# A hybrid decoder layer on one core: v buffers with names of their own, more u units in the selection, another order at both ends, and a decay mask on ScalarE and VectorE

## The chip, the cores and the metric

The kernel runs on one core of a Trainium2 chip. The metric is the time of one execution on the device in microseconds (us). A profile of one execution goes with it: a span from the first to the last instruction, and a record of each instruction on the engines PE (TensorE; PEld is its weight load), DVE (VectorE), ACT (ScalarE), POOL (GpSimd) and on the DMA queues, of which SP (SyncE) issues nearly all loads.

## The reference

One decoder layer in float32 on 512 tokens of width 1024:

```python
n = rmsnorm(x)                                   # one projection feeds both mixers
h = x + W_out @ concat(gla(n), ssd(n))           # gated linear attention; Mamba-2 SSD
n2 = rmsnorm(h)
# PEER: 8 heads, product keys 128 x 128 = 16384 experts, the top 16 per head
q  = n2 @ w_query;  best 16 of each key half, then best 16 of their 256 sums, gate = softmax
h += sum_e gate[e] * gelu(n2 . u[e]) * v[e]
y  = rmsnorm_final(h)

# in ssd, per chunk of 128 tokens and per head
a_cum = cumsum(dt * A)
Lmat  = exp(where(causal, a_cum[l] - a_cum[s], -inf))     # the decay matrix
y_diag = ((C @ B.T) * Lmat) @ (X * dt)
```

## The kernel before

Each engine runs its instructions in the order in which the program was written, so the order of the code is the schedule. Where precision asks for it, an operand is split into a rounded high part and the rest: `split` (L102 to L104) makes the high part on ACT and the rest on DVE or, on request, on POOL, and `mm3` (L108 to L110) does three matmuls with the parts.

The stages, with their place in the profile:

- **Start (0 to 16 us).** The tokens are normalised (`scale`, L242; the power on POOL, L235), transposed (L266) and multiplied with 23 blocks of `w_in` that arrive one after another as `wraw`. `ahead` splits a block early.
- **Mixers (16 to 225 us).** In the SSD part `ssd_a(t)` makes, for each of 4 chunks and two groups of 4 heads, the decay matrix `lm`: matmuls with `selH` (L566) spread the cumulated decay over a PSUM bank, one matmul of `identr` with `negm` (L568) adds a large negative number above the diagonal, and ACT takes the exponential with a bias for each head (L571, `b<-pm,RT` in the profile). DVE then multiplies `lm` with the scores `psc` (L602, `b<-b,pm`), and `ssd_b(t)` uses it on PE (L614).
- **Query and selection (to 466 us).** DVE sorts out the top 16 of 16 and builds one-hot tables: `select` has chains of `tensor_tensor` on f16, which read and write `gat`. PE in the meantime does u units: one unit (`u_run(1)`) is 24 matmuls of a 128-expert block of `uT` with the tokens, whose raw block `ur` is loaded by SP and split by ACT and, in this stage, by POOL (`ul<-ur,uh`). `spread` transposes the indices on PE.
- **Gate stage (466 to 656 us).** 48 units `gunit`, 8 tokens each, make the dense gate matrix with one-hot matmuls from tables `A`, `eq`, `B` that DVE builds (L1186, `pg<-B,A`). The gates of the first 59 expert blocks stay in the `ring`; those of the others go to DRAM (`gd`) from the tile `stage`, 64 tokens at a time, by six DMAs on ACT's queue (L1199). The u units that are left are spread over these units in eight parts each, split on ACT and DVE: 33 units before.
- **V stage (to 1487 us).** One step for each of 128 expert blocks `e`: load v (`vr`, four buffers) and split it, split the gated activations of the ring slot (`hh`, `hl`), multiply, and do one u unit for a later block. `gload` refills a ring slot from `gd`. 256 gathers for the last 128 tokens are threaded in on POOL.
- **End.** `final()` (L1257 to L1320) adds the residuals and applies the last norm, four tiles of 128 tokens, to the output.

Which engine waits for a buffer is decided by the tile pools: a tile whose address was used by another tile waits for the last user of that one. The loads at the change from the gate stage to the V stage stand in this order:

```python
vs = Stream(self, vp, "v", [...], 4)
HT[0] = htile()
vs.loads(1)          # v blocks 0 and 1
u_run(1)
vs.split(1)
hprep(0)
u_run(1)
vs.loads(3)
...
gload(RS)            # first ring refill
```

Of the kernel before, what the change touches and what calls it, by code (L numbers as in the profile page):

```python
# [35 lines left out]
class Stream:  # L36
# [10 lines left out]
    def loads(s, upto):  # L47
        while s.nl <= min(upto, len(s.src) - 1):
            s.raw[s.nl] = s.c.tile([128, 1024], F32, name=s.nm + "r", bufs=s.nraw)
            s.y.load(s.raw[s.nl], s.src[s.nl])  # L50
            s.nl += 1
# [12 lines left out]
class Layer:  # L64
# [67 lines left out]
    def mixers(self):  # L132
# [125 lines left out]
        scale(2, 1, False)  # L258
        scale(3, 0, True)
# [7 lines left out]
        for dc in range(8):  # L267
            if dc == 0:
                ahead(0, 3, 0)
            act(nh[dc], px[dc], AF.Copy, scale=wmix[:, dc:dc + 1])  # L270
            stt(nl[dc], px[dc], wmix[:, dc:dc + 1], nh[dc].bitcast(F32), OP.mult, OP.subtract)
            if dc == 4:
                ahead(0, 3, 1)
        negm = c.tile([128, 128], F32R, name="negm")
        identr = c.tile([128, 128], F32R, name="identr")
        V.tensor_copy(negm, negm0)
        V.tensor_copy(identr, ident)
# [56 lines left out]
        def dts():  # L334
# [20 lines left out]
            V.tensor_scalar(R[32:40, :], ac, -1.0, None, op0=OP.mult)  # L355
# [9 lines left out]
        nacT = lambda t: RT[:, t, 32:40]  # L365
# [193 lines left out]
        def ssd_a(t):  # L559
            ts = slice(t * 128, (t + 1) * 128)  # L560
            lm = b4(F32, (128, 8, 128))
            for g in range(2):
                p = pt()
                for j in range(4):
                    h = 4 * g + j
                    T.matmul(p[:, j * 128:(j + 1) * 128], selH[:, h:h + 1].to_broadcast([40, 128]), acs[:, ts],  # L566
                             start=j == 0, stop=False, skip_group_check=True)
                T.matmul(p, identr, bc(negm, 1, 4), start=False, stop=True, skip_group_check=True)  # L568
                for j in range(4):
                    h = 4 * g + j  # L570
                    act(lm[:, h, :], p[:, j * 128:(j + 1) * 128], AF.Exp, bias=nacT(t)[:, h:h + 1])  # L571
# [27 lines left out]
            for g in range(2):  # L599
                r = slice(g * 64, g * 64 + 64)  # L600
                T.matmul(psc[g][:, :128], XB[4][r, ts], XB[5][r, ts], start=True, stop=True)
                tt(lm[:, 4 * g:4 * g + 4, :], lm[:, 4 * g:4 * g + 4, :], bc(psc[g][:, :128], 1, 4), OP.mult)  # L602
# [255 lines left out]
    def experts(self):  # L858
# [237 lines left out]
        select(1)  # L1096
        spread(0)
        u_run(1)
# [10 lines left out]
        u_run(4)  # L1109
# [124 lines left out]
        vs.loads(1)  # L1234
# [4 lines left out]
        vs.loads(3)  # L1239
# [15 lines left out]
        gload(RS)  # L1255

        def final():  # L1257
# [3 lines left out]
            junk = [c.tile([128, D], F32, name="gat", tag="gat", bufs=3), vp.tile([128, D], F32, name="vr", bufs=4)]  # L1261
# [26 lines left out]
            def scale(t):  # L1288
                stt(hs[t], hs[t], v[t][:, 3:4], wf, OP.mult, OP.mult)
                load(self.out[t], hs[t])  # L1290
# [9 lines left out]
            scale(3)  # L1300
            mean(0)
            power(0)
            residual(1, 0)
            weight(1, 0, G)
            residual(1, 1)
            weight(1, 1, G)
            scale(0)
            mean(1)
            power(1)
            residual(2, 0)  # L1310
            weight(2, 0, G)
            residual(2, 1)
            weight(2, 1, V)
            act(hs[1], hs[1], AF.Copy, scale=v[1][:, 3:4])
            load(self.out[1], hs[1])
            mean(2)
            power(2)
            act(hs[2][:, hf[0]], hs[2][:, hf[0]], AF.Copy, scale=v[2][:, 3:4])
            V.tensor_scalar(hs[2][:, hf[1]], hs[2][:, hf[1]], v[2][:, 3:4], None, op0=OP.mult)
            load(self.out[2], hs[2])  # L1320

        for e in range(NE):
# [8 lines left out]
            vs.loads(e + 4)  # L1331
# [15 lines left out]
            for i in range(3):  # L1347
                vgrp(0, i)
                if i == 2:
# [3 lines left out]
                    gload(e + 1 + RS)  # L1353
# [3 lines left out]
            for i in range(3):  # L1357
# [5 lines left out]
                fill(3 + i)  # L1363
            u_part(7)
            fill(6)
            if e == NE - 12:
                for t in (0, 1):
                    hs[t] = us.c.tile([128, D], F32, name="ur", bufs=2)
                    load(hs[t], self.hd[t])
# [99 lines left out]
```

## Time and profile before

| what | value |
|---|---|
| three runs, us | 1506.76, 1508.53 (median), 1512.19 |
| the profiled execution, us | 1503.02 |
| its span, us | 1501.2 |
| mean granted TensorE clock | 0.991 |
| busy, us: PE, PEld | 1456.2, 1278.0 |
| busy, us: DVE, ACT, POOL | 1169.4, 632.7, 451.7 |
| chain that ended last | PE 80%, DVE 12%, issue 3%, DMA 2%, ACT 2% |

The span lies 1.8 us under the execution's own time. Busy times of engines lie beside each other, and matmuls are pipelined, so the duration of a matmul in a row is longer than its distance to the next one. The chain is followed back from the last instruction, at each step to what released it.

### The profile page before, as it was taken

The numbers are of one execution on the slowest core, as the hardware profiler recorded it, in microseconds if no ns is written. First come the engines' busy times: TensorE is split into PE (matmuls) and PEld (weight loads), VectorE is DVE, ScalarE is ACT, GpSimd is POOL, SyncE is SP. The second block draws the span as 40 slices with busy tenths as digits, with TensorE's granted clock in tenths as the row PEclk, the third lists the DMA queues.
The fourth block names the chain that finished last, engine by engine and source line by source line (L and its number), as shares of the span: only waits on it lengthen the run. The fifth ranks groups of instructions, "written<-read, shape, count | busy, mean of one in ns | idle before, by whom it ended". The sixth has DMA issues, their size and how long they took to land.

```text
span 1501.2 us, 22402 instructions
## 1 busy us (share of the span) xinstructions
PE 1456.2 (97%) x7904; PEld 1278.0 (85%) x7904; DVE 1169.4 (78%) x2473; ACT 632.7 (42%) x1201; POOL 451.7 (30%) x380
## 2 busy tenths in 40 slices
PE   7999999999898999979999999999999999999997
PEld 5787778888898999878999999999999998888886
DVE  6542663789999999967877778777788888888886
ACT  5435633433654544433333333333333333444444
POOL 2002404444672000002333333333333333333332
PEclk9999999999999999999999999999999999999999
DMA  5231224222334556658888888889899888888894
GB/s 189 84 126 58 71 73 155 96 85 85 105 104 143 159 167 175 180 181 300 322 316 316 323 312 307 317 305 332 304 331 322 314 316 276 292 300 299 297 325 178
DMA packets 148738, 335.56 MB, mean 224 GB/s; under 512 B 64640, under 2 KB 73872, under 8 KB 148496
## 3 DMA queue, kind: packets, MB, share of 16 engines
q1 hardware_dynamic: 58672, 186.32, 36.1%
q0 software_dynamic: 36864, 134.23, 25.1%
q10 hardware_dynamic: 53088, 13.57, 3.9%
q8 instruction: 62, 1.02, 0.3%
q14 instruction: 52, 0.43, 0.1%
HBM read 315.79 MB, written 18.28 MB: 223 GB/s over the span
## 4 chain that ended last, share of the span: by engine, by line
PE 80%; DVE 12%; issue 3%; DMA 2%; ACT 2%; POOL 0%; SPq 0%; DVEq 0%; POOLq 0%; ACTq 0%
PE pm L109 25%; PE pm L108 25%; PE pm L110 25%; DVE gat L97 4%; PE pg L1186 2%; DVE B L97 1%; DVE ul L104 1%; PE pm L904 1%; DMA gd<-stage 1%; DVE ring L97 1%; DMA ur<-in_uT 1%; DVE eq L97 1%; DVE A L97 1%; ACT b L91 0%; ACT tp L91 0%
## 5 line engine op out<-in xcount | busy, mean ns | idle before, releaser
L108 PE MATMUL pm<-nT,uh 128*128 128x384 f32 (+1 forms) x1152 | 402.1, 349 | 8.8 <-ACT uh L91 8.3
L110 PE MATMUL pm<-nT,ul 128*128 128x384 f32 (+1 forms) x1152 | 397.0, 345 | 2.0 <-POOL ul L104 2.0
L109 PE MATMUL pm<-nT,uh 128*128 128x384 f32 (+1 forms) x1152 | 397.0, 345 | 0.5 <-DVE nT L97 0.5
L109 PE MATMUL pm<-vl,hh 128*128 128x512 f32 x765 | 300.4, 393 | 0.2 <-DVE vl L104 0.2
L110 PE MATMUL pm<-vh,hl 128*128 128x512 f32 x765 | 300.3, 393 | 0.0
L108 PE MATMUL pm<-vh,hh 128*128 128x512 f32 x765 | 299.0, 391 | 0.2 <-ACT vh L91 0.2
L1135 POOL DMA_INDIRECT gat<-in_u,idx x128 | 136.8, 1069 | 473.3 <-DVE gat L100 467.0
L91 ACT ACTIVATE uh<-ur 128x512 fp32r<-128x512 f32 x288 | 180.2, 629 | 214.1 <-PE pm L109 182.0
L108 PEld LDWEIGHTS pm<-nT,uh 128*128 128x128 f32 x1152 | 218.1, 189 | 33.5 <-ACT uh L91 8.7
L109 PEld LDWEIGHTS pm<-nT,uh 128*128 128x128 f32 x1152 | 218.1, 189 | 25.0 <-DVE nT L97 1.1
L110 PEld LDWEIGHTS pm<-nT,ul 128*128 128x128 f32 x1152 | 217.7, 189 | 9.1 <-POOL ul L104 2.9
L1135 POOL DMA_INDIRECT gat<-in_v,idx x128 | 147.2, 1150 | 253.1 <-DVE n2a L100 220.4
L91 ACT ACTIVATE vh<-vr 128x512 fp32r<-128x512 f32 x255 | 159.4, 626 | 136.8 <-PE pm L110 135.4
L104 DVE TENSOR_TENSOR vl<-vr,vh 128x512 fp32r<-128x512 f32 x255 | 175.3, 688 | 37.4 <-ACT vh L91 36.4
L104 DVE TENSOR_TENSOR ul<-ur,uh 128x512 fp32r<-128x512 f32 x206 | 140.7, 689 | 56.8 <-ACT uh L91 56.4
L100 DVE SCALAR_TENSOR_TENSOR n2a<-gat,dots,n2a 128x1024 f32<-128x1024 f32 x128 | 164.0, 1281 | 21.5 <-DMA gat<-in_v,idx 18.5
L110 PEld LDWEIGHTS pm<-vh,hl 128*128 128x128 f32 x765 | 143.7, 188 | 30.9
L100 DVE SCALAR_TENSOR_TENSOR gat<-gat,n2a 128x1024 f32<-128x1024 f32 x128 | 156.2, 1220 | 9.8 <-DMA gat<-in_u,idx 9.6
L108 PEld LDWEIGHTS pm<-vh,hh 128*128 128x128 f32 x765 | 144.0, 188 | 14.2 <-ACT vh L91 0.7
L109 PEld LDWEIGHTS pm<-vl,hh 128*128 128x128 f32 x765 | 144.0, 188 | 14.1 <-DVE vl L104 0.5
L104 POOL TENSOR_TENSOR ul<-ur,uh 128x512 fp32r<-128x512 f32 x82 | 118.7, 1455 | 99.8 <-ACT uh L91 99.4
L91 ACT ACTIVATE gl<-pm 128x384 f32<-128x384 f32 (+16 forms) x104 | 46.0, 442 | 219.8 <-PE pm L110 219.8
(254 smaller groups left out, 1685.2 us busy)
## 6 DMA issues: line engine op xcount, KB each, us to landing
ur<-in_uT SPq DMA_DIRECT2D x128, 512.0 KB, 6.0
vr<-in_v SPq DMA_DIRECT2D x128, 512.0 KB, 5.0
gd<-stage ACTq DMA_DIRECT2D x6, 2208.0 KB, 14.5
ring<-gd SPq DMA_DIRECT2D x69, 192.0 KB, 5.2
wraw<-in_w_in SPq DMA_DIRECT2D x23, 512.0 KB, 4.4
ur<-in_w_query SPq DMA_DIRECT2D x16, 512.0 KB, 3.7
b<-in_x SPq DMA_DIRECT2D x8, 512.0 KB, 3.6
wraw<-in_w_out SPq DMA_DIRECT2D x8, 512.0 KB, 3.9
```

The lines of the kernel that those rows point to most:

```text
L91: return self.S.activation(out, in_, f, **k)
L97: return self.V.tensor_tensor(out, x, y, op=op)
L100: return self.V.scalar_tensor_tensor(out, x, s, y, op0=op0, op1=op1, **k)
L104: (self.G if pool else self.V).tensor_tensor(lo, src, hi.bitcast(F32), op=OP.subtract)
L108: T.matmul(out, lhi, rhi, start=start, stop=False)
L109: T.matmul(out, lhi, rlo, start=False, stop=False)
L110: T.matmul(out, llo, rhi, start=False, stop=stop)
L904: T.matmul(p[:, t * 128:(t + 1) * 128], q[:, t * 128:(t + 1) * 128], skT[:, b, :], start=True, stop=True)
L1135: G.indirect_dma_start(out=r, out_offset=None, in_=src, in_offset=bass.IndirectOffsetOnAxis(ap=idx[:, k:k + 1], axis=0))
L1186: T.matmul(o, A[:, t // 2, :, t % 2], B[:, i, t // 2, :, t % 2], start=i == 0, stop=i == 1)
```

## The change

Five places are edited. The raw buffers of a stream get names of their own (`vr0` to `vr3`, `ur0`, `ur1`, with one buffer each), where one name had several buffers before; three v blocks are asked for ahead of the u units at the change of stages, not two, and the ring refills and the fourth v block later. One u unit more stands before `spread(0)` in the selection and one more behind `spread(2)`, and one stands on the other side of `spread(0)`. The decay matrix is made as exp(-relu(acum[s] - acum[l])) with no mask matmul, and the scores are multiplied with a 0/1 matrix `causal` before they meet it. At the start the split of block 0 is written ahead of the last `scale`, at the end `final()` is in another order, with `scale` in halves and the last store in two.

```diff
     def loads(s, upto):
         while s.nl <= min(upto, len(s.src) - 1):
-            s.raw[s.nl] = s.c.tile([128, 1024], F32, name=s.nm + "r", bufs=s.nraw)
+            s.raw[s.nl] = s.c.tile([128, 1024], F32, name=f"{s.nm}r{s.nl % s.nraw}", bufs=1)
             s.y.load(s.raw[s.nl], s.src[s.nl])
...
         scale(2, 0, False)
         power(vs_[3])
         scale(2, 1, False)
+        parts[0] = b4(F32R), b4(F32R)
+        for k in range(2):
+            f = slice(k * 512, k * 512 + 512)
+            act(parts[0][0][:, f], raws[0][:, f], AF.Copy)
+        for k in range(2):
+            f = slice(k * 512, k * 512 + 512)
+            self.G.tensor_tensor(parts[0][1][:, f], raws[0][:, f], parts[0][0][:, f].bitcast(F32), op=OP.subtract)
+        raws.pop(0)
+        seen[1] = 1
         scale(3, 0, True)
         scale(3, 1, False)
...
         for dc in range(8):
-            if dc == 0:
+            if dc == 1:
                 ahead(0, 3, 0)
             act(nh[dc], px[dc], AF.Copy, scale=wmix[:, dc:dc + 1])
             stt(nl[dc], px[dc], wmix[:, dc:dc + 1], nh[dc].bitcast(F32), OP.mult, OP.subtract)
             if dc == 4:
                 ahead(0, 3, 1)
-        negm = c.tile([128, 128], F32R, name="negm")
-        identr = c.tile([128, 128], F32R, name="identr")
-        V.tensor_copy(negm, negm0)
-        V.tensor_copy(identr, ident)
+        causal = negm0
+        V.tensor_scalar(causal, negm0, 0.0, None, op0=OP.is_ge)
...
-            V.tensor_scalar(R[32:40, :], ac, -1.0, None, op0=OP.mult)
+            V.tensor_copy(R[32:40, :], ac)
...
-        nacT = lambda t: RT[:, t, 32:40]
+        acT = lambda t: RT[:, t, 32:40]
...
-                             start=j == 0, stop=False, skip_group_check=True)
-                T.matmul(p, identr, bc(negm, 1, 4), start=False, stop=True, skip_group_check=True)
+                             start=True, stop=True)
+
                 for j in range(4):
                     h = 4 * g + j
-                    act(lm[:, h, :], p[:, j * 128:(j + 1) * 128], AF.Exp, bias=nacT(t)[:, h:h + 1])
+                    act(lm[:, h, :], p[:, j * 128:(j + 1) * 128], AF.Relu, scale=-1.0, bias=acT(t)[:, h:h + 1])
+                act(lm[:, 4 * g:4 * g + 4, :], lm[:, 4 * g:4 * g + 4, :], AF.Exp, scale=-1.0)
...
-                tt(lm[:, 4 * g:4 * g + 4, :], lm[:, 4 * g:4 * g + 4, :], bc(psc[g][:, :128], 1, 4), OP.mult)
+                ms = c.tile([128, 128], F32, name="ms", bufs=2)
+                tt(ms, psc[g][:, :128], causal, OP.mult)
+                tt(lm[:, 4 * g:4 * g + 4, :], lm[:, 4 * g:4 * g + 4, :], bc(ms, 1, 4), OP.mult)
...
         select(1)
+        u_run(2)
         spread(0)
-        u_run(1)
         ties(3)
...
         spread(2)
-        u_run(4)
+        u_run(5)
         spread2(2)
...
-        vs.loads(1)
+        vs.loads(2)
         u_run(1)
         vs.split(1)
         hprep(0)
         u_run(1)
-        vs.loads(3)
...
-        gload(RS)
...
-            def scale(t):
-                stt(hs[t], hs[t], v[t][:, 3:4], wf, OP.mult, OP.mult)
-                load(self.out[t], hs[t])
+            def scale(t, cols=slice(0, D)):
+                stt(hs[t][:, cols], hs[t][:, cols], v[t][:, 3:4], wf[:, cols], OP.mult, OP.mult)
 
             square(3, 0)
             square(3, 1)
@@ -1298,26 +1304,29 @@
             residual(0, 0)
             residual(0, 1)
             scale(3)
+            load(self.out[3], hs[3])
             mean(0)
             power(0)
             residual(1, 0)
             weight(1, 0, G)
+            scale(0, hf[0])
             residual(1, 1)
-            weight(1, 1, G)
-            scale(0)
+            residual(2, 0)
+            scale(0, hf[1])
+            load(self.out[0], hs[0])
+            residual(2, 1)
             mean(1)
             power(1)
-            residual(2, 0)
-            weight(2, 0, G)
-            residual(2, 1)
-            weight(2, 1, V)
-            act(hs[1], hs[1], AF.Copy, scale=v[1][:, 3:4])
-            load(self.out[1], hs[1])
+            scale(1, hf[1])
             mean(2)
             power(2)
+            act(hs[1][:, hf[0]], hs[1][:, hf[0]], AF.Copy, scale=v[1][:, 3:4])
+            load(self.out[1], hs[1])
+            weight(2, 0, V)
             act(hs[2][:, hf[0]], hs[2][:, hf[0]], AF.Copy, scale=v[2][:, 3:4])
-            V.tensor_scalar(hs[2][:, hf[1]], hs[2][:, hf[1]], v[2][:, 3:4], None, op0=OP.mult)
-            load(self.out[2], hs[2])
+            self.S.dma_start(self.out[2][:, hf[0]], hs[2][:, hf[0]])
+            scale(2, hf[1])
+            load(self.out[2][:, hf[1]], hs[2][:, hf[1]])
...
-            vs.loads(e + 4)
+            vs.loads(e + 4 if e else 2)
...
-                    gload(e + 1 + RS)
+                    if e:
+                        gload(e + 1 + RS)
...
+            if e == 0:
+                gload(RS)
+                gload(RS + 1)
```

The instructions move as follows on three queues. On SP, at the change from the gate stage to the V stage; `vr` are raw v blocks, `ur` raw u blocks, `ring` the refills from `gd`, and the brackets name the semaphores that each load waits for (DMAHW are DMAs that have landed). Before:

```order
L88 DMA ur_6891<-in_uT 128x1024 [waits DMAHW1_49,DVE_49]
L88 DMA vr_6961<-in_v 128x1024 [waits DMAHW6_49,PE_49]
L88 DMA vr_6963<-in_v 128x1024 [waits DMAHW4_49,Activation_49]
L88 DMA ur_6966<-in_uT 128x1024 [waits DMAHW2_49,DVE_49]
L88 DMA ur_7012<-in_uT 128x1024 [waits DMAHW3_49,DVE_49]
L88 DMA vr_7049<-in_v 128x1024
L88 DMA vr_7051<-in_v 128x1024
L88 DMA ring_2196<-gd_64 128x384 [waits DVE_49]
L88 DMA vr_7064<-in_v 128x1024 [waits DMAHW5_49]
L88 DMA ur_7070<-in_uT 128x1024 [waits DMAHW7_49,DVE_49]
L88 DMA ring_2196<-gd_64 128x384 [waits DMAHW6_49,DVE_49]
```

and in the change:

```order
L88 DMA ur0_6900<-in_uT 128x1024 [waits DMAHW1_49,DVE_49]
L88 DMA vr0_6970<-in_v 128x1024 [waits DMAHW6_49,PE_49]
L88 DMA vr1_6972<-in_v 128x1024
L88 DMA vr2_6974<-in_v 128x1024
L88 DMA ur1_6977<-in_uT 128x1024 [waits DMAHW2_49,DVE_49]
L88 DMA ur0_7023<-in_uT 128x1024 [waits DMAHW3_49,DVE_49]
L88 DMA ur1_7074<-in_uT 128x1024 [waits DMAHW0_49,DVE_49]
L88 DMA ring_2211<-gd_64 128x384 [waits DMAHW4_49]
L88 DMA ring_2211<-gd_64 128x384 [waits DVE_49]
L88 DMA vr3_7146<-in_v 128x1024 [waits DMAHW5_49]
L88 DMA vr0_7148<-in_v 128x1024 [waits DMAHW6_49]
```

The second v load has lost its waits, a third stands behind it, and the wait on DMAHW4 that it had now stands at the first ring refill, behind three u loads. On PE, at the first `ssd_a`; `acum,selH` are the spread decays, `negm,identr` the mask, `ea,selE` what follows. Before:

```order
L566 MATMUL pm<-acum,selH 128x128 x4
L568 MATMUL pm<-negm,identr 128x512
L566 MATMUL pm<-acum,selH 128x128 x4
L568 MATMUL pm<-negm,identr 128x512
L575 MATMUL pm<-ea,selE 128x128 x4
```

and in the change:

```order
L573 MATMUL pm<-acum,selH 128x128 x8
L583 MATMUL pm<-ea,selE 128x128 x4
L586 MATMUL pm<-ident,b_627 128x128 x2
L586 MATMUL pm<-ident,b_628 128x128 x2
L602 MATMUL pm<-ident,b_629 128x128
```

The two mask matmuls are gone, and what followed them stands directly behind the eight of `selH`. On POOL, the last instructions of the program, in `final()`; the powers are those with `mhalf`, `ur` and `gat` are the tiles being weighted. Before:

```order
L1286 TENSOR_TENSOR rs_14557<-rs_14557,mhalf 128x1
L1286 TENSOR_TENSOR rs_14554<-rs_14554,mhalf 128x1
L1279 TENSOR_TENSOR ur<-ur,gat 128x512 x2
L1286 TENSOR_TENSOR rs_14555<-rs_14555,mhalf 128x1
L1279 TENSOR_TENSOR gat<-gat 128x512
L1286 TENSOR_TENSOR rs_14556<-rs_14556,mhalf 128x1
```

and in the change:

```order
L1293 TENSOR_TENSOR rs_14566<-rs_14566,mhalf 128x1
L1293 TENSOR_TENSOR rs_14563<-rs_14563,mhalf 128x1
L1286 TENSOR_TENSOR ur_14233<-ur_14233,gat 128x512
L1293 TENSOR_TENSOR rs_14564<-rs_14564,mhalf 128x1
L1293 TENSOR_TENSOR rs_14565<-rs_14565,mhalf 128x1
```

POOL has one product where it had three, and none between the last two powers.

## Rows read from the trace of the kernel before

**Rows 1.** What PE waited for, whole span: us in total, times, longest

```profile
PE pg L1186 <- DVE B L97: 8.6, 18, 3.3
PE pm L108 <- ACT uh L91: 8.3, 1, 8.3
```

**Rows 2.** Windows: busy us of each engine (instructions), PE clock, DMA share, GB/s

```profile
core 0: us, PE busy (x) PEld busy (x) DVE busy (x) ACT busy (x) POOL busy (x), PEclk, DMA share, GB/s
...
670.00:678.00 8.00, 2.35 (x6) 1.92 (x7) 2.37 (x5) 2.98 (x6) 0.00 (x0) 0.50 0.88 343
678.00:680.00 2.00, 2.00 (x7) 1.73 (x7) 2.00 (x4) 0.00 (x0) 0.59 (x1) 0.61 0.95 366
...
1000.00:1100.00 100.00, 100.00 (x507) 90.49 (x506) 79.48 (x130) 37.48 (x73) 34.42 (x32) 1.00 0.90 321
```

**Rows 3.** Timeline of SP's queue, 640 to 690 us: start, us, what

```profile
652.55 17.66 SPq L88 DMA_DIRECT2D vr<-in_v  x2
670.30 0.86 SPq L88 DMA_DIRECT2D ur<-in_uT  x2
```

**Rows 4.** The chain that ended last, 640 to 690 us

```profile
656.49 13.32 DMA gd<-stage
```

**Rows 5.** Timeline of PE, 664 to 681 us; brackets: idle before, releaser

```profile
675.65 0.69 PE L108 MATMUL pm<-nT,uh 128*128 128x384 f32 x1 [8.26 <-ACT uh L91]
```

**Rows 6.** Timeline of DVE, 650 to 700 us

```profile
657.78 0.69 DVE L104 TENSOR_TENSOR ul<-ur,uh 128x512 fp32r<-128x512 f32 x1 [0.66 <-ACT uh L91]
...
660.98 0.69 DVE L104 TENSOR_TENSOR ul<-ur,uh 128x512 fp32r<-128x512 f32 x1 [0.29 <-ACT uh L91]
```

**Rows 7.** DMA issues, 558 to 575 us: count, KB each, median to landing

```profile
ur<-in_uT SPq DMA_DIRECT2D x3, 512.0 KB, 6.7
```

**Rows 8.** Line 568 (duration min/median/max), and PE's timeline behind the first

```profile
L568 PE MATMUL pm<-negm,identr x8: 494/502/503, 172.4 to 211.7; 128*128 128x512 f32 x8
...
172.81 0.66 PE L566 MATMUL pm<-acum,selH 40*128 40x128 f32 x4
```

**Rows 9.** Groups by shape, 160 to 216 us: busy, mean ns, idle before

```profile
L91 ACT ACTIVATE b<-pm,RT 128x128 f32<-128x128 f32 x32 | 8.7, 379 | 1.9 <-PE pm L568 1.9
L91 ACT ACTIVATE tp<-tp 128x512 f32<-128x512 f32 x3 | 1.9, 631 | 7.2 <-DVE tp L97 7.2
...
L100 DVE SCALAR_TENSOR_TENSOR tp<-b,d_skip,pm 128x128 f32<-128x128 f32 x12 | 3.4, 343 | 1.5 <-PE pm L614 1.5
```

**Rows 10.** Timelines of DVE and PE, 171 to 181 us

```profile
176.39 1.27 DVE L97 TENSOR_TENSOR b<-b,pm 128x512 f32<-128x512 f32 x2
...
178.46 1.09 PE L614 MATMUL pm<-b,tp 128*64 128x128 f32 x16
```

**Rows 11.** Timelines of DVE and POOL, 392 to 466 us

```profile
422.96 1.47 DVE L97 TENSOR_TENSOR gat<-gat 128x1024 f16<-128x1024 f16 x3
...
429.26 4.41 DVE L97 TENSOR_TENSOR gat<-gat 128x1024 f16<-128x1024 f16 x3
...
426.46 7.07 POOL L104 TENSOR_TENSOR ul<-ur,uh 128x512 fp32r<-128x512 f32 x4 [0.55 <-ACT uh L91]
```

**Rows 12.** Gate stage: windows as in Rows 2, and a group of DVE

```profile
462.00:470.00 8.00, 6.96 (x51) 6.67 (x51) 6.25 (x11) 2.08 (x4) 2.06 (x3) 0.79 0.62 202
...
600.00:656.00 56.00, 52.89 (x436) 49.39 (x434) 55.39 (x96) 24.99 (x65) 1.15 (x1) 1.00 0.55 162
...
L104 DVE TENSOR_TENSOR ul<-ur,uh 128x512 fp32r<-128x512 f32 x63 | 42.0, 684 | 3.8 <-ACT uh L91 3.7
```

**Rows 13.** Start: timelines of POOL and PE, and a piece of the chain

```profile
13.67 2.37 POOL L104 TENSOR_TENSOR b<-wraw,b 128x1024 fp32r<-128x1024 f32 x1 [1.78 <-DMA d_skip<-in_d_skip]
...
16.09 0.50 PE L110 MATMUL pm<-nT,b 128*128 128x512 f32 x1 [0.35 <-POOL b L104]
...
23.78 4.48 DMA wraw<-in_w_in
```

**Rows 14.** End: timelines of POOL and of SP's queue

```profile
1495.01 1.40 POOL L1279 TENSOR_TENSOR gat<-gat 128x512 f32<-128x512 f32 x1
...
1497.70 0.33 SPq L88 DMA_DIRECT2D out_dram<-gat  x1
```

More of the change, by code (lines that the diff above doesn't have):

```diff
@@ L1260, in final @@
             hf = [slice(0, 512), slice(512, 1024)]
-            junk = [c.tile([128, D], F32, name="gat", tag="gat", bufs=3), vp.tile([128, D], F32, name="vr", bufs=4)]
+            junk = [c.tile([128, D], F32, name="gat", tag="gat", bufs=3), vp.tile([128, D], F32, name=f"vr{NE % 4}", bufs=1)]
             v = [nv() for _ in range(4)]
@@ L1367, in experts @@
                 for t in (0, 1):
-                    hs[t] = us.c.tile([128, D], F32, name="ur", bufs=2)
+                    hs[t] = us.c.tile([128, D], F32, name=f"ur{t}", bufs=1)
                     load(hs[t], self.hd[t])
```

## The prediction

> **What bounds the kernel now.** I read the page first, then the table of what TensorE waited for, then windows over the stages where those waits lie. The page's busy line has PE at 1456.2 of 1501.2 us, so the whole kernel holds about 45 us in which PE does nothing, and any gain must come from those 45 us, from work taken off PE, or from stages where another engine sets the pace. The reader is to see in the waits that the gate stage (waiting for `B` of DVE) and one single wait for `uh` of 8.3 us hold most of the idle time that has a name inside the program [rows 1]. The V stage, from about 680 us to the end, is solid: 100.00 us of PE in 100, at a DMA share of 0.90 [rows 2]. The change does not alter its steady state, so what can be won lies before it and in the last microseconds.
>
> The 8.3 us wait is at the transition from the gate stage to the V stage. PE sits for 8.26 us until 675.65 [rows 5], and comes back at a granted clock of 0.50, later 0.61 [rows 2]. SP's queue tells why: the row from 652.55 holds two v loads over 17.66 us, and the u loads behind them are issued only at 670.30 [rows 3]; the chain passes at that place through the store of the last gates, 13.32 us [rows 4]. SP stood at the second v load until that store was done, since the buffer it was given overlaps the stage tile being stored, and the u block that PE needed stood behind it.
>
> **The change part by part.** Durations are of the profiled execution (1503.02 us, span 1501.2). It lies 5.5 us under the median of the three runs, 1508.53; I take the sum from the span and subtract it from the median.
>
> **Transition.** The v buffers now have rising addresses and three of them are free of the stage tile, so SP issues three v loads at once and reaches the u loads, which wait for nothing but the DVE splits of the u units before. Those end at 657.78 + 0.69 = 658.5 and 660.98 + 0.69 = 661.7 [rows 6]. During an earlier gate store u loads landed in a median of 6.7 us [rows 7], so the first would be there at 665.2, and converted by ACT (0.63, the 128x512 form of [rows 9]) at 665.8. PE runs out of work at 675.65 - 8.26 = 667.4. The idle 8.26 then goes. So does the time lost to the low clock: 2.35 us of PE at 0.50 and 2.00 at 0.61 [rows 2] are 2.4 us of full-speed work in 4.35, which gives 1.95 back. Together 10.2. Against it stand the two extra v loads, 1 MB, ahead in the same queue: at the 321 GB/s of the V stage they are 3.3 us, and most of that lies before the store starts to move. If all of it came on top, u would land at 668.5 and PE would wait some 2 us. The ring loads and the fourth v load wait for the store behind those u loads; the products that need them have a unit's time of slack. I take **-9.5** (from -5 to -10.2).
>
> **Decay mask.** Eight mask matmuls go: their own time is 0.50 each [rows 8], but the first starts at 172.4 and the next PE instruction stands at 172.81, so each takes about 0.42 of the line, 3.4 in all, from a stage where PE has no gap. ACT replaces 32 Exp of 128x128 by as many Relu, at equal shape equal at 379 ns, and adds eight Exp of 128x512 at 0.63: 5 us [rows 9]. Relu between Exps might ask for activation table loads; the built program has eight, as before, so I count none. DVE adds eight 128x128 products from PSUM, bounded by 0.34 (a two-operand instruction of that shape, [rows 9]) and by nothing: at most 2.7 us. Both are hidden as long as the decay matrix is ready when PE comes to `ssd_b`. The tightest place is t=0: DVE ends at 176.39 + 1.27 = 177.66 and PE starts there at 178.46 [rows 10], 0.8 us of cover. After, PE is 0.84 earlier, and DVE, which starts on a PE result, too, but has 0.7 more to do: cover about 0.1. The three others start later in their PE work. I take **-3.4**, from -1 (t=0 and one more give half back) to -4 (all of the 0.50).
>
> **Selection.** Two u units move from the gate stage to the selection. There PE has room, since it waits on DVE for its transposes and DVE runs nearly without a gap, so PE's own work for them is covered. But a unit there splits on Pool, and this is where the change costs something. The three adds of a select take DVE 1.47 us with Pool quiet and 4.41 while Pool runs four splits in 7.07 us [rows 11]: 2.94 us for about 2.4 splits, 1.2 us for each. Two units are four splits, 4.9 at most; some of DVE's instructions there are of kinds that did not stretch, so +3.5. In return, the gate stage has 31 units to compute, not 33. DVE is busy 55.39 of 56.00 us at its end, and sets the pace; a unit there is two splits of 0.684 and a short product [rows 12], 3 us for two. At its start DVE is busy only 6.25 of 8, with the PE clock at 0.79, after PE's wait [rows 12]; a PE kept busy may save 1.5 of that. Net **-1**, from -6 (Pool's splits fall beside nothing that stretches) to +2 (all stretch and the start stays).
>
> **Start.** The split of block 0 is issued before the last scale. Pool's part began at 13.67 and took 2.37, and PE waited 0.35 for it at 16.09 [rows 13]. In halves from about 12 us on it is done before PE wants it, and ACT's part no longer stands ahead of the first nT. That is 0.7 to 1.1 us for PE, but the chain takes a w_in load of 4.48 at 23.78 [rows 13] that this does not move at its full length: **-0.7** (0 to -1.1).
>
> **End.** Pool's last weight product of 1.40 at 1495.01 is on the chain, and the store is issued at 1497.70 [rows 14]. After, DVE makes it, and the last power on Pool no longer stands behind it: 1.40 sooner, less some 0.6 for a half scale of 128x512 that DVE now does ahead of the mean that the power reads, so 0.8. The last rows go out as two half stores on two queues, which may save 0.4 more: **-1.2** (0 to -2).
>
> Sum: 9.5 + 3.4 + 1 + 0.7 + 1.2 = 15.8. Span 1501.2 - 15.8 = 1485.4, profiled run 1487.2, median 1508.5 - 15.8 = **1492.7**.
>
> **The rivals.** *The transition stall moves instead of going.* If u lands behind the three v loads and most of the store, as late as the store's end at 669.8 plus its own conversion, PE still waits some 3 to 4 us and falls to the low clock for a few: the term is -4.5, the time 1497.7. For it: the DMA engines are near full while the store moves. Against it: u loads issued in the middle of earlier stores landed in 6.7.
>
> *Pool's splits hold DVE.* All four splits stretch DVE's instructions by 1.2, and PE's wait at the gate stage's start stays, because DVE comes later to the first `B`: 4.9 - 3 = +2, the time 1495.7. For it: every add beside Pool splits took three times its short time [rows 11]. Against it: nothing, but part of the splits may fall beside short instructions. The Trainium skill, "SBUF — State Buffer", section "Who interferes with whom", gives a rule of this kind: a VectorE instruction with two SBUF inputs contends with a GpSimd instruction that reads SBUF, and the one that comes second blocks for the whole instruction. By that rule, which the 1.47 against 4.41 bears out, the two units are not worth moving, and the time would be this rival's.
>
> *The mask gives nothing.* The longer chain of Relu, Exp and product reaches PE late in all four `ssd_b`: the 3.4 are given back, 1496.1. For it: the cover of 0.1 at t=0. Against it: the other places have more.
>
> *Slower: the V stage loses step.* With the v and u buffers fixed in rotation and the ring load started a block later, a load could come late for each block. There are 127 blocks, so from 0.16 us a block (20 us) on the change is slower than before; at 0.2 it would be 1518. For it: the DMA share of 0.90 leaves little. Against it: PE stands in no gap there now [rows 2], and from the second block on SP's order is the old one.
>
> **How the numbers follow.** Chances: forecast 0.68; transition 0.14; Pool 0.12; mask 0.03; V stage 0.03. Of single runs of this kernel 0.3%, 4.5 us, is about what can be told from no change. The forecast's own range is 1488 to 1497. Low end: the best bounds of the transition, the mask and the selection together would be 1486.4; I take 1485. High end: the transition rival and the Pool rival together give 1500.7; I take 1502. Faster needs less than 1504.0: all but the V stage's case and the worst sums of several rivals, 0.91; same 0.06; slower 0.03.
>
> **What would show it.** Transition: SP issues three v loads together near 653, u near 658 and 662, and PE's wait for `uh` falls from 8.3 to under 2. Mask: no line of the mask, and no PE wait for `b` of DVE at `ssd_b`. Selection: the first gate product about 3.5 us later against the start of the selection than before, and a gate stage shorter by 4 to 5. End: the last store issued within 0.9 us less after the last matmul. What would make the forecast wrong is a u load that lands after 670, a first gate product that comes 5 us late, or gaps of PE in the V stage.

## The result and the profile after

The changed kernel takes 1489.74 us (median of four runs, 1488.34 to 1492.24) against 1507.87 for the kernel before (1506.76 to 1512.19): ratio 0.9876, 95% interval 0.9852 to 0.9901. That is 18.1 us; I had said 15.8 and 1492.7. The profiled executions lie closer together: spans of 1488.9 and 1501.2, 12.4 us. The difference of 5.7 is no rounding, and it is told below.

The table gives the length of each stage, from the start of one instruction to that of another in the traces. Stages: up to the first spread matmul of SSD; from there to the last `ssd_b` group; first query matmul to the first gate product; first to last gate product; from there to the 13th high-part matmul of the V stage; from there to the last matmul; from there to the last store that SP issues.

| stage | before | after | difference | the prediction's term |
|---|---|---|---|---|
| start and mixers | 171.78 | 170.87 | -0.91 | -0.7 |
| SSD | 48.92 | 49.00 | +0.08 | -3.4 |
| query and selection | 221.38 | 224.31 | +2.93 | +3.5 |
| gate stage | 192.89 | 188.42 | -4.47 | -4.5 |
| transition | 38.04 | 27.67 | -10.37 | -9.5 |
| V stage | 799.02 | 799.03 | +0.01 | 0 |
| end | 5.14 | 5.18 | +0.04 | -1.2 |

The differences add up to -12.7. Two stretches stand outside the table: from the last `ssd_b` to the first query matmul (20.5 in both), and from the last store's issue to the end of the span, 3.55 before and 3.87 after. With that +0.3 they make the 12.4 of the spans.

What PE waited for, over the whole span of the changed kernel (us in total, times, longest):

```profile
PE pg L1196 <- DVE B L97: 8.4, 24, 1.3
PE pm L275 <- ACT b L91: 7.5, 1, 7.5
PE pm L110 <- POOL ul L104: 3.0, 4, 1.0
PE pm L1027 <- DVE ii L97: 1.3, 1, 1.3
PE pm L659 <- ACT b L91: 1.0, 1, 1.0
PE pm L609 <- ACT b L91: 0.9, 2, 0.5
```

Against [rows 1] the 8.3 us for `uh` are gone, and two lines have come that were not there: PE waits at lines 609 and 659 for the instructions of ACT that write `b`, the decay matrix (with 0.6 at line 108, which is not shown, 2.5 in all). Windows of the same kernel (columns as in [rows 2]):

```profile
662.00:670.00 8.00, 8.00 (x44) 7.39 (x43) 5.65 (x10) 4.49 (x9) 0.70 (x1) 1.00 1.15 348
670.00:678.00 8.00, 8.00 (x42) 7.31 (x41) 5.81 (x12) 3.09 (x6) 2.17 (x3) 1.00 0.88 306
1000.00:1100.00 100.00, 100.00 (x506) 90.58 (x506) 79.47 (x127) 37.48 (x73) 34.89 (x31) 1.00 0.91 323
```

PE is busy through the transition at a granted clock of 1.00, where it had stood and then run at 0.50 (the lower of its two levels, 1.2 GHz) and 0.61. SP's queue shows why (start, us, what):

```profile
650.17 1.33 SPq L88 DMA_DIRECT2D vr<-in_v  x3
656.12 9.01 SPq L88 DMA_DIRECT2D ur<-in_uT  x3
671.04 0.80 SPq L88 DMA_DIRECT2D ring<-gd  x2
```

Three v loads go out within 1.33 us, and the u loads follow at 656.12, 14 us ahead of [rows 3]. The first landed after 6.6 us, as the 6.7 of [rows 7] had it.

In the SSD stage, timelines of ACT and PE of the changed kernel at the second chunk (start, us; brackets: idle before, releaser):

```profile
179.50 1.12 ACT L91 ACTIVATE b<-pm,RT 128x128 f32<-128x128 f32 x4
180.65 0.63 ACT L91 ACTIVATE b<-b 128x512 f32<-128x512 f32 x1
181.19 1.12 ACT L91 ACTIVATE b<-pm,RT 128x128 f32<-128x128 f32 x4
...
180.68 0.65 PE L609 MATMUL pm<-b 64*128 64x128 f32 x4 [0.54 <-ACT b L91]
182.37 0.88 PE L659 MATMUL pm<-tp,on 128*128 128x128 f32 x4 [1.04 <-ACT b L91]
```

The reader is to see that neither PE instruction reads the decay matrix: line 609 makes the scores from the convolved inputs, which are tiles of the name `b` as well, and line 659 belongs to the norm of the chunk before. They write PSUM banks, and each starts within 0.06 us of the end of a group of four Relu (179.50 + 1.12 = 180.62, 181.19 + 1.12 = 182.31). Each group reads one bank, and in the program the two matmuls are given these two banks next. The Exp of the first group stands ahead of the second group's Relu, and holds the second bank longer.

In the selection, timelines of DVE and POOL:

```profile
460.35 1.79 DVE L97 TENSOR_TENSOR A<-itx,i2s 128x1024 f16<-128x1024 f16 x1
462.06 1.78 DVE L97 TENSOR_TENSOR eq<-itx,i1s 128x1024 f16<-128x1024 f16 x1
...
465.16 0.74 DVE L97 TENSOR_TENSOR A<-itx,i2s 128x1024 f16<-128x1024 f16 x1
...
460.31 1.28 POOL L104 TENSOR_TENSOR ul<-ur,uh 128x512 fp32r<-128x512 f32 x1 [1.28 <-ACT uh L91]
```

The first tables `A` and `eq` take 1.79 and 1.78 beside the two splits of the fifth unit, and the second `A` 0.74 without; before, the first two took 0.69 each.

The last microseconds, timelines of DVE and POOL:

```profile
1482.04 0.75 DVE L100 SCALAR_TENSOR_TENSOR ur<-ur,rs,gat 128x512 f32<-128x512 f32 x1 [0.66 <-POOL rs L1293]
1482.71 0.15 DVE L1289 TENSOR_SCALAR rs<-rs 128x1 f32<-128x1 f32 x1
1482.96 0.21 DVE L1290 TENSOR_SCALAR rs<-rs 128x1 f32<-128x1 f32 x1
1483.09 0.68 DVE L1286 TENSOR_TENSOR gat<-gat 128x512 f32<-128x512 f32 x1
...
1483.25 0.93 POOL L1293 TENSOR_TENSOR rs<-rs,mhalf 128x1 f32<-128x1 f32 x1 [1.25 <-DVE rs L1290]
```

The mean of tile 2 (1482.71) stands behind a scale of tile 1, which waits for Pool's power of tile 1. The last power starts at 1483.25 for that reason. Of the 1.40 of [rows 14] only 0.4 is gained: it starts 3.44 us behind the last matmul, and started 3.82 behind it before. That is lost again: beside DVE's product (1483.09) the power takes 0.93, and it took 0.54 before.

### The profile page after: what moved, and what is told of

It reads as the page before. It is cut to its first block, busy times and chain, and to the rows that moved or that the text cites. A ratio compares the mean times of both kernels' runs of the same rounds, so it can differ in the third digit from the quotient of the medians.

```text
span 1488.9 us, 22403 instructions
## 1 busy us (share of the span) xinstructions
PE 1453.5 (98%) x7896; PEld 1276.4 (86%) x7896; DVE 1174.1 (79%) x2476; ACT 636.2 (43%) x1208; POOL 456.2 (31%) x383
## 4 chain that ended last, share of the span: by engine, by line
PE 79%; DVE 14%; issue 3%; ACT 2%; DMA 2%; POOL 0%; DVEq 0%; POOLq 0%; SPq 0%; ACTq 0%
PE pm L109 25%; PE pm L108 25%; PE pm L110 25%; DVE gat L97 4%; DVE B L97 1%; PE pg L1196 1%; DVE ul L104 1%; ACT b L91 1%; DVE eq L97 1%; DVE A L97 1%; DVE ring L97 1%; DMA ur<-in_uT 1%; PE pm L914 1%; ACT tp L91 0%; PE pm L275 0%
## 5 line engine op out<-in xcount | busy, mean ns | idle before, releaser
L104 POOL TENSOR_TENSOR ul<-ur,uh 128x512 fp32r<-128x512 f32 x86 | 124.9, 1461 | 98.6 <-ACT uh L91 95.7
L91 ACT ACTIVATE gl<-pm 128x384 f32<-128x384 f32 (+15 forms) x102 | 45.4, 445 | 220.1 <-PE pm L110 220.1
```

The lines of the kernel that those rows point to most:

```text
L91: return self.S.activation(out, in_, f, **k)
L104: (self.G if pool else self.V).tensor_tensor(lo, src, hi.bitcast(F32), op=OP.subtract)
```

## The experiments

The stages of the runs, as in the table above (SSD, query and selection, gate stage, transition, V stage, end):

| kernel | SSD | selection | gates | transition | V stage | end | time, median (runs) |
|---|---|---|---|---|---|---|---|
| names_only | 50.09 | 221.49 | 193.36 | 29.65 | 809.86 | 5.13 | 1503.82 (1499.16 to 1507.62) |
| order_only | 48.88 | 220.51 | 193.18 | 40.64 | 807.36 | 5.13 | 1514.08 (1508.43 to 1517.83) |
| mask_only | 49.00 | 220.55 | 193.33 | 39.14 | 807.09 | 5.14 | 1510.89 (1503.90 to 1513.15) |
| mask_late_exp | 47.68 | 220.59 | 194.28 | 38.14 | 804.73 | 5.14 | 1508.01 (1500.44 to 1511.33) |
| sel_only | 53.52 | 225.04 | 186.02 | 37.71 | 805.89 | 5.13 | 1508.12 (1500.81 to 1511.03) |
| after_again | 50.26 | 224.17 | 186.41 | 27.67 | 799.07 | 5.15 | 1488.74 (1488.30 to 1489.38) |
| after_late_end | 47.68 | 224.28 | 185.90 | 27.67 | 799.02 | 4.27 | 1486.01 (1485.39 to 1489.86) |
| after_late_end_fill | 54.88 | 224.17 | 186.49 | 27.67 | 799.03 | 4.27 | 1492.32 (1489.96 to 1498.95) |
| after_no_mask | 47.36 | 224.34 | 186.84 | 27.67 | 799.03 | 5.18 | 1492.58 (1487.69 to 1495.10) |
| after_no_sel | 49.07 | 220.44 | 194.23 | 27.67 | 799.04 | 5.18 | 1493.33 (1490.98 to 1493.95) |
| after_stall | 50.03 | 224.17 | 186.53 | 27.67 | 823.29 | 5.18 | 1513.44 (1509.77 to 1516.52) |
| sel_no_pool | 50.16 | 215.93 | 185.92 | 27.67 | 799.03 | 5.18 | 1480.63 (one run) |

The kernel before, run beside them, had medians of 1509.56 (first four), 1509.49 (next four) and 1512.46 (last four), and was spread from 1500.48 to 1516.38. With that spread the medians of single parts say little; the stages say more.

**names_only**: the kernel before with the names of the raw buffers.

```diff
-            s.raw[s.nl] = s.c.tile([128, 1024], F32, name=s.nm + "r", bufs=s.nraw)
+            s.raw[s.nl] = s.c.tile([128, 1024], F32, name=f"{s.nm}r{s.nl % s.nraw}", bufs=1)
```

> Kernel before with one part of the change: the raw buffers have names of their own (rising addresses), the order of the loads is the old one. Theory: the buffer's address alone caused the stall, since the second v load then waits for nothing, so the whole 10.4 us that the transition gave in the changed kernel is here: time 10 us under before (ratio about 0.9933), PE's wait for uh at the change of stages under 1 us. Rival: the later ring loads are needed as well, because a v load and a ring load still stand at the gate store ahead of other loads; then half of it, about 5 us.

Its ratio is 0.9963 (0.9939 to 0.9987). The transition is 29.65 in the table, which looks like 8.4 of the 10.4 us. PE's wait for `uh` is gone; in its place, from 655 to 720 us, stand

```profile
PE pm L108 <- ACT hh L91: 1.8, 1, 1.8
PE pm L109 <- DVE vl L104: 1.0, 1, 1.0
```

with SP's next pair of v loads held for 11.85 us by the store. The first of these waits ends at 687.11 with the 13th high-part matmul itself, so the table's boundary cuts the new stall in two: the second wait, and a stretch at the lower clock behind it (0.83 granted from 685 to 695), are counted in the V stage. Up to the 19th high-part matmul, behind the stall, it is 46.36 us from the last gate product in the kernel before, 40.85 here and 35.99 in the changed kernel. So the addresses did 5.5 us and the order of the loads the other 4.9: the rival's half, and not the theory's whole.

**order_only**: the kernel before with the order of the loads.

```diff
-        vs.loads(1)
+        vs.loads(2)
...
-        vs.loads(3)
...
-        gload(RS)
```

> Kernel before with the other part: three v loads asked for at once, ring loads and the fourth v load later, buffers as before. Theory: the second v load still gets the buffer under the stage tile and waits for the store with the u loads behind it, so the stall of 8.3 us stays and the time is that of before within 1 us. Rival: the order is what frees the u loads; then 5 to 10 us less.

Ratio 1.0026 (1.0001 to 1.0050). The stall is there, longer than before:

```profile
PE pm L108 <- ACT uh L91: 10.0, 1, 10.0
```

Three v loads now stand ahead of the late u loads. The theory's stall is met, its "within 1 us" is not: alone, the order costs 2.6 us of transition in this profile; with the names it gives 4.9.

**mask_only**: the kernel before with the mask on ScalarE and VectorE, as in the diff of the change.

> Kernel before with the decay mask on ScalarE and VectorE alone. The changed kernel reached the end of the SSD stage no earlier than before. Theory: PE, 0.87 us earlier in each chunk, now meets PSUM banks that the longer ACT chain (Relu, Exp, Relu) frees later, waits some 2.5 us there and loses clock, which eats the 3.4 us of the removed matmuls: 0 us against before (between -1 and +1). Rival: the part brings its 3.4 us and the loss in the changed kernel came from another place: -3.4 us.

Ratio 0.9997 (0.9975 to 1.0019), the SSD stage 49.00 against 48.92, with PE's waits of 1.0 and 0.9 at the same two instructions as in the changed kernel. The theory's number and its place are met in the profile; the total alone could not tell 0 from the rival's -3.4 (a ratio of 0.9977).

**mask_late_exp**:

```diff
-                act(lm[:, 4 * g:4 * g + 4, :], lm[:, 4 * g:4 * g + 4, :], AF.Exp, scale=-1.0)
+            for g in range(2):
+                act(lm[:, 4 * g:4 * g + 4, :], lm[:, 4 * g:4 * g + 4, :], AF.Exp, scale=-1.0)
```

> As the mask alone, but both Exps stand behind both groups of Relu, so the second PSUM bank of a chunk is read 0.53 us sooner; the decay matrix of the first group is ready 1.1 us later. Theory (banks are what PE waits for): 0.5 us less wait in three chunks and less time at low clock, 1.5 to 2.5 us faster than the mask alone. Rival (the finished decay matrix is late): no gain or a loss of up to 1 us, with PE waiting for DVE at ssd_b.

The SSD stage is 47.68, 1.3 us under the mask alone, and again 47.68 in after_late_end: a little under what was expected. All of PE's waits in the stage are 2.0 us, not 2.5, and the stage's mean granted clock is 0.96, not 0.93. The ratio, 0.9985 (0.9958 to 1.0012), cannot tell it.

**sel_only**: the kernel before with the three lines of the selection.

```diff
+        u_run(2)
         spread(0)
-        u_run(1)
...
-        u_run(4)
+        u_run(5)
```

> Kernel before with two more u units in the selection alone. In the changed kernel the first gate product came 2.1 us later than before although the stages ahead were 0.85 earlier, and the end of the gate stage was then 1.55 us better than those stages explain. Theory (Pool's splits hold DVE and the fifth unit at the end delays the first gate table, given back by a shorter gate stage): first gate product 2.5 to 3.5 us later, last one 1 to 2 us earlier than in the kernel before, the total 1 to 2 us less. Rival (the gain at the gate stage came from the changed SSD and start): last gate product no earlier.

Selection +3.66, gates -6.87, together -3.2, more than expected. The total (ratio 0.9993, 0.9965 to 1.0020) does not show it: this profile's SSD stage, which the edit does not touch, is 53.52, at a granted clock of 0.86 from 170 to 182 us and 0.79 from 182 to 198; and its V stage is 6.9 us longer.

**after_again**: the changed kernel, no edit.

> The changed kernel once more on the chip of the runs beside it. From its trace against that of before up to the V stage and behind it: 12.5 us less than before, ratio 0.9917; the first timing gave 18 us, which I take to be partly the difference of executions in the V stage. If instead the change reaches into the V stage, the ratio is again near 0.988.

Ratio 0.9863 (0.9826 to 0.9899): near the first timing, not at 0.9917. Its six runs lie within 1.1 us, the 17 of the kernel before beside them within 15.6. So the difference of the medians is there again, and the stages of the two profiles do not hold it. That it lies in the V stage, in executions of the kernel before that were not profiled, is the guess that after_stall goes after.

**after_late_end**: the changed kernel with the late Exps, and

```diff
-            scale(1, hf[1])
             mean(2)
             power(2)
+            scale(1, hf[1])
```

> The changed kernel with both Exps behind both groups of Relu, and at the end the mean and power of tile 2 ahead of the scale of tile 1. Theory: SSD stage 1 to 1.5 us shorter than in the changed kernel (bank waits), the last store 0.7 to 1.3 us earlier against the last matmul, since the last mean no longer waits behind a scale that waits for Pool: 2 to 2.5 us under the changed kernel. Rival: the end is set by DVE's total work, so that the order does not matter: end unchanged.

1486.01 against 1488.74 beside it, ratio to before 0.9851 (0.9813 to 0.9888). SSD 47.68 (1.3 us under the first profile of the changed kernel, 2.6 under after_again), and the end 4.27 in place of 5.15: the end as expected, SSD at least so. Timelines of DVE, ACT and SP:

```profile
1477.93 0.14 DVE L1290 TENSOR_SCALAR rs<-rs 128x1 f32<-128x1 f32 x1
1478.48 0.21 DVE L1291 TENSOR_SCALAR rs<-rs 128x1 f32<-128x1 f32 x1 [0.41 <-ACT gat L91]
...
1480.72 0.33 SPq L88 DMA_DIRECT2D out_dram<-gat  x1
```

The second mean now waits for ACT's square alone, and 1480.72 - 1478.48 is all that follows. Five of its six runs lie under all of the changed kernel's: this version beats both kernels.

**after_late_end_fill**:

```diff
-        ssd_c(0)
         wo(4)
         op(0,0,(0,))
+        ssd_c(0)
```

and the same for `ssd_c(1)` and `op(2,0,(1,))`.

> As the run before it, and the output matmuls that stood behind ssd_c in two chunks stand ahead of it, so that PE has work while ACT makes the decay matrix. Theory (PE idles for ACT there, and loses clock): 1 to 2 us less in the SSD stage than without it, no PE wait for b of ACT at the norm matmul. Rival: those matmuls wait for their weights or take the banks that ssd_c needs, no gain or a loss.

A miss: SSD 54.88. In its place, from 165 to 245 us,

```profile
PE pm L108 <- ACT b L91: 4.6, 4, 2.5
```

and the longest of these waits, in timelines of ACT and PE:

```profile
191.35 0.63 ACT L91 ACTIVATE b<-tp 128x512 fp32r<-128x512 f32 x1 [2.12 <-DVE tp L100]
192.04 0.50 PE L108 MATMUL pm<-b,b 128*128 128x512 f32 x1 [2.46 <-ACT b L91]
```

The output matmul behind `ssd_c` waits for the high part of what `ssd_c` has just normalised, and once more at 212.63, for 1.4 us. The matmuls that were moved ahead had covered that wait. The rival had the loss, by another cause than its weights or banks.

**after_no_mask**: the changed kernel with the decay matrix as before.

```diff
+                T.matmul(p, identr, bc(negm, 1, 4), start=False, stop=True, skip_group_check=True)
...
-                    act(lm[:, h, :], p[:, j * 128:(j + 1) * 128], AF.Relu, scale=-1.0, bias=acT(t)[:, h:h + 1])
-                act(lm[:, 4 * g:4 * g + 4, :], lm[:, 4 * g:4 * g + 4, :], AF.Exp, scale=-1.0)
+                    act(lm[:, h, :], p[:, j * 128:(j + 1) * 128], AF.Exp, bias=nacT(t)[:, h:h + 1])
```

> The changed kernel with the mask matmuls put back, all else changed. Theory (the mask part is worth nothing, since PE then waits at PSUM banks): same time as the changed kernel, 1488 to 1490, the SSD stage from its first spread matmul to its last ssd_b 49 to 50 us in both. Rival (it is worth the 3.4 us of the matmuls, hidden in the earlier runs by differences of clock): 1492.

Inconclusive. The median 1492.58 is the rival's; its ratio to the kernel before on its own chip, 0.9872 (0.9848 to 0.9896), is that of the changed kernel; and the SSD stage of its profile, 47.36, is shorter than with the mask. That stage without the mask part is 47.36, 48.88, 48.92, 50.09 and 53.52 in five profiles, with it 49.00 to 50.26 in six. What differs most is the granted clock. In after_no_mask it is 1.00, with PE at work throughout,

```profile
198.00:206.00 8.00, 8.00 (x71) 6.13 (x70) 7.13 (x17) 3.36 (x10) 0.00 (x0) 1.00 0.00 0
```

and in the changed kernel

```profile
198.00:206.00 8.00, 7.13 (x50) 5.38 (x50) 6.96 (x17) 4.95 (x13) 0.04 (x1) 0.79 0.03 10
```

The whole stage at the same granted clock of 0.93, in the changed kernel and in names_only (columns as in [rows 2]):

```profile
170.87:219.87 49.00, 46.46 (x308) 36.27 (x307) 33.16 (x80) 25.76 (x67) 1.10 (x2) 0.93 0.16 55
172.01:222.10 50.09, 50.09 (x316) 38.01 (x315) 31.10 (x72) 21.03 (x59) 1.10 (x2) 0.93 0.15 53
```

PE has 3.6 us less work with the part and stands 2.5 us, so 1.1 are left. The stages order themselves by clock: without the part 1.00 (47.36), 0.97 (48.88, 48.92), 0.93 (50.09) and 0.87 (53.52); with it, as in the change, 0.93 (49.00, 49.00, 49.07) and 0.90 (50.03 to 50.26). The part is worth some 1 us at an equal clock, by three profiles against one, and none of the six with it had more than 0.93. Whether PE's waits bring the clock down is not shown: in sel_only it fell to 0.87 without one.

**after_no_sel**:

```diff
-        u_run(2)
         spread(0)
+        u_run(1)
...
-        u_run(5)
+        u_run(4)
```

> The changed kernel with the u units of the selection as before. Theory: from the first query matmul to the last gate product the changed kernel takes 3.5 us less than before (first gate product 3.5 us later, gate stage 7 us shorter); so this one is 3 to 4 us slower than the changed kernel, 1492 to 1493. Rival (the term of 1 us in the prediction): 1490.

1493.33, ratio 0.9871 (0.9845 to 0.9898); its selection and gates take 414.67 against 410.58 to 412.73 in the changed kernel. 2 to 4 us: the theory by its stages. Its time cannot be held against the changed kernel's directly, since another chip ran it.

**after_stall**:

```diff
             s.y.split(hi, lo, s.raw[i][:, k * 512:(k + 1) * 512], pool)
+            if s.nm == "v" and s.ns == 60:
+                for _ in range(30):
+                    s.y.V.tensor_tensor(lo, s.raw[i][:, k * 512:(k + 1) * 512], hi.bitcast(F32), op=OP.subtract)
```

> The changed kernel with one stall made in the V stage: VectorE writes the low part of one half v block 30 times more, some 18 us, so PE runs dry once near block 30 and its clock falls. In the profiles so far a V stage takes 8.32 or 8.44 us a block, and the pace changed only where PE had stood still; the kernels with a stall at the transition were spread over 15 us, the changed kernel over 1 us. Theory (the pace is drawn anew when PE comes back from a stall): times 13 to 20 us longer, and spread over 4 us or more, with blocks at 8.44 behind the stall in some executions. Rival (the pace belongs to the buffers or the order of the loads): 8.32 behind the stall in each, spread about 1 us.

Windows ahead of the stall, in it, and behind it:

```profile
850.00:900.00 50.00, 50.00 (x254) 45.31 (x253) 39.95 (x70) 18.58 (x36) 17.24 (x17) 1.00 0.89 310
920.00:940.00 20.00, 9.77 (x37) 8.60 (x38) 18.46 (x31) 1.15 (x2) 2.71 (x3) 0.61 0.36 115
...
1000.00:1050.00 50.00, 50.00 (x250) 45.04 (x249) 39.36 (x67) 18.59 (x36) 16.63 (x16) 1.00 0.86 303
```

PE is full and the clock 1.00 on both sides, yet it gets through 254 matmuls in 50 us ahead and 250 behind. A block takes 8.32 us up to the stall, the block of the stall 27.99, and each one behind it with a u unit 8.44. The theory's pace is met in this one profile, and the rival's 8.32 is not: a stall can change the pace. The V stage is 24.3 us longer than without the stall, 19.7 in the stalled block and 4.6 in the 38 slower ones, more than the theory's 13 to 20. The spread decides nothing. The twelve runs lie within 6.75 us and the six of after_again within 1.1, but the first four of the changed kernel lie within 3.9, and after_no_mask (7.4) and after_late_end_fill (9.0) are spread as far without a stall in the V stage of their profiles.

**sel_no_pool**:

```diff
-            s.y.split(hi, lo, s.raw[i][:, k * 512:(k + 1) * 512], pool)
+            if pool and getattr(s, "nolo", False):
+                s.y.act(hi, s.raw[i][:, k * 512:(k + 1) * 512], AF.Copy)
+                lo = hi
...
+        us.nolo = True
```

> The changed kernel with the splits on Pool in the selection left out: the u units there use the high part in place of the low part, so the output is not the reference's. Theory (Pool's splits hold VectorE's two-input instructions): the three adds of each select take 1.47 us in all eight places, not 4.4, and VectorE's work from the first one-hot table to the last index falls from 63 us by 15 us or more; PE then sets the pace there. Rival (the long adds come from something else, such as the loads): they stay at 4.4.

Timeline of DVE, two of the eight groups of adds, the others read the same:

```profile
404.99 1.48 DVE L101 TENSOR_TENSOR gat<-gat 128x1024 f16<-128x1024 f16 x3
431.46 1.48 DVE L101 TENSOR_TENSOR gat<-gat 128x1024 f16<-128x1024 f16 x3
```

In the changed kernel six of the eight take 4.38 to 4.42. DVE's stretch from the first table to the last index falls from 62.99 us (396.22 to 459.21) to 40.80. The stage gets only 8.2 us of that (215.93 against 224.17). PE then sets the pace: it was busy 30.00 of 30.00 us from 395 to 425, where it is busy 27.38 in the changed kernel. The Trainium skill, "SBUF — State Buffer", section "Who interferes with whom", has the rule; these rows agree with it.

## Why the prediction was right, and where it was wrong

**Start: right in the traces.** PE's 0.35 us for Pool's split [rows 13] are gone, and the first of those matmuls starts at 14.48, not at 15.01: -0.91 for -0.7. No run has this part alone.

**Transition: right.** The u load landed 6.6 us after its issue, where 6.7 was used; the stall and the low clock went, 10.37 for -9.5. The two extra v loads cost nothing that shows. names_only and order_only say which half of the edit did it: 5.5 by the addresses, 4.9 by the order on top of them, and the order alone makes it worse.

**Selection and gate stage: right in sign, the pieces near.** +2.93 for +3.5, -4.47 for -4.5. In the later profiles of the changed kernel the gate stage gave more (186 against 193), so the net of -1 is under-sized: -1.5 to -3.7. The rival on Pool's splits is true as a mechanism (sel_no_pool), but a split costs DVE less than 1.2 when it falls in a place that is stretched anyway. From its first table to its last index DVE took 62.28 us before and 62.99 after, so the unit that was added there moved which adds are long and cost 0.7. The other 2.2 are the first `A` and `eq`, 1.1 for each split of the fifth unit, near the 1.2 that was used.

**Mask: wrong.** The step that failed is "both are hidden as long as the decay matrix is ready when PE comes to `ssd_b`". The matrix was ready: PE has no wait at `ssd_b`, so the sign that was named for this term came true without its gain. What PE met was the PSUM bank that ACT had not read out yet, at instructions that have nothing to do with the matrix by their data. I asked what reads the new result, not what the longer chain keeps hold of. Eight mask matmuls went, but 2.5 us of waits and a granted clock of 0.93 in place of 0.97 came. The term was 0 in the profile, as the third rival had it, by another cause than that rival's.

**End: wrong.** "So 0.8" counted the product off Pool and a half scale onto DVE, but not that this scale waits for a power, with the last mean queued behind it. after_late_end, which swaps the two, gives 0.9. The "0.4 more" for two half stores on two queues did not come either: what follows the last store's issue is 0.3 longer.

**V stage: the total came out by luck.** The sum of terms that can be compared is 12.7 in the traces for 15.8 predicted, and the measured 18.1 holds 5.4 us that no term had. For its profiled execution the changed kernel had a forecast of 1487.2, and took 1490.63: 3.4 us too long, the size of the mask's term. I read the 5.5 us between the profiled execution and the median of before as an offset that both kernels share. It is not: the changed kernel's profiled execution lies 0.9 above its median. The likely cause is the pace. The kernel before may come out of its stall at either of two paces; its profiled execution had the faster; the changed kernel has no stall there, and both its profiles keep the faster one. A whole V stage at the slower pace is 8.1 us longer (mask_only, 807.09), enough for the 5.4. That a stall can change the pace is shown by after_stall and names_only, in which blocks of 8.32 stand ahead of the stall and of 8.44 behind it. That the kernel before runs at the slower one in its other executions is not shown, since none of them was profiled, nor that this makes up the whole 5.4 us.

## What to carry to other kernels

Where a removed instruction gave PE a few tenths of a microsecond ahead of an engine that frees its PSUM banks, look at who reads those banks last, and move work that holds them (here an Exp) behind the reads. Two tiles whose lifetimes meet at a stage's end should not share addresses: one load that waits for an old store holds every load behind it on its queue. Free addresses and the order of the loads each gave about half here. And when runs spread more than the profile explains, compare the profiled execution with the median before trusting a sum made from it.

## What the runs showed of the hardware

PE has two paces at the same granted clock of 1.00. In profiles the V stage takes 8.32 or 8.44 us a block of 42 matmuls, 1.4% apart, and holds it for hundreds of microseconds; the later blocks, without a u unit, take 4.08 in every profile. All seven profiled kernels that came to the V stage without a stall and had none in it (the changed kernel twice, after_late_end, after_late_end_fill, after_no_mask, after_no_sel, sel_no_pool) ran at 8.32; of those that had one, the kernel before kept 8.32, the other six (names_only, order_only, mask_only, mask_late_exp, sel_only and after_stall) were at 8.44 behind it for long stretches. In sel_only and mask_late_exp it went back to 8.32 at the same block, the 50th, which took 9.54 and 8.39 us there. In sel_only PE waited 0.72 us at that block; in mask_late_exp the trace shows no wait of PE there. So the pace did not change only where PE had stood still, as the expectation of after_stall has it. What in the chip sets it stays open.
